# Weight sums of a Strassen feed-forward made earlier and in half-size pieces, and buffers at the change of products given out in order of release

## The chip, the core and the metric

The kernel runs on one core of a Trainium2 chip. TensorE (PE) multiplies matrices into PSUM, VectorE (DVE) and ScalarE (ACT) work on tiles in SBUF, GpSimd (POOL) and SyncE (SP) here mostly issue transfers between device memory and SBUF. Each engine works through its own instructions in the order of the program and waits for others by semaphores. The metric is device time in microseconds.

## The reference

One layer of a hybrid decoder, for 1024 prompt tokens and 8 sample tokens with the same weights; the model width is 1024, the feed-forward width 4096.

```python
y_a, hT_re, hT_im = s5_mixer(u_a, h0_re, h0_im, ...)
v_b = layer_norm(v_b, sgu_ln_g, sgu_ln_b)
y_b = u_b * spatial_mix(v_b, sgu_w, sgu_b)
merged = (jax.nn.sigmoid(gate_a) * (y_a @ w_branch_a)
          + jax.nn.sigmoid(gate_b) * (y_b @ w_branch_b))
mix = merged @ w_out + b_out
x1 = layer_norm(DN_ALPHA * x + mix, ln1_g, ln1_b)
ff = jnp.square(jax.nn.relu(x1 @ w_up + b_up)) @ w_down + b_down
ple = jax.nn.sigmoid(x1 @ w_ple_gate + b_ple_gate) * (p @ w_ple)
x2 = layer_norm(DN_ALPHA * x1 + ff + ple, ln2_g, ln2_b)
```

## The kernel before

Activations are held transposed, 128 features by 1032 tokens to a tile. For precision each operand is split into a high part (written by ACT) and a low part (a DVE subtraction), and a product takes three matmuls. `raw` is a weight tile as it is loaded, `hl` its two parts, `hraw` and `hop` the same for hidden activations that come back from memory.

The program goes through these stages: input projection, state-space scan and gates (to 376 us in the profiled execution); the spatial gating (`sgu_head`, whose last output is `ubt[3]`); `glu`; the merge of the two branches (8 m's, `pab`, evacuated by DVE as `sb` and `sa`); the output projection in two passes over token halves; the gate of the per-layer embedding `pg(0, m)`, then `pg(1, m)`, which also makes the operands `xT`, `xb` of the feed-forward; the up stage from 715 us; the down stage from 1070 us; the last layer norm.

Both feed-forward products are one level of Strassen: seven products instead of eight. In the up stage `up_pair(p)` runs 16 times. Each pair has seven products of 24 matmuls of 128 x 128 x 258 twice; UPO gives their order. ACT or DVE reads each product out of PSUM into `pu`, `p5`, `hA` or `hB`; `hA` and `hB` are squared after a relu, combined into `tA` and `tB`, and stored to `hd` by POOL's queue. Products that share the PSUM region `a` follow each other only after the one ahead is read out. `up_ahead` makes the weights of a coming product: `up_prep` loads both halves of `w_up` and forms the sums (`raw` of 128 x 512), then `split`.

The down stage needs sums of its own weights, S1 to S4, as well. `dn_sums` makes them: for k = 0 to 7 it loads tiles `x`, `y` (`dsum`) and `z` (`dsz`) of 128 x 1024, adds and subtracts four times on DVE, and stores each result with POOL's queue to device memory, from where the down stage loads them. It is a generator: every `next(dsums, None)` in `up_pair` lets it go on for one step. A list scheduler then fixes the order on each engine, so that the order below, not the place in the code, says where an instruction stands.

At the change from up to down, `acc2tags`, `rtags` and `ntags` say which SBUF tiles become the accumulators `acb` (loaded by SP), the four `hraw` buffers and the 23 `hop` tiles. They are taken from a fixed list.

Of the kernel before, what the change touches and what calls it, by code (L numbers as in the profile page):

```python
# [57 lines left out]
def hybrid_step_kernel(ctx: ExitStack, tc: tile.TileContext, i, o):  # L58
# [13 lines left out]
    psb = psb_ctx.enter_context(tc.tile_pool(name="psb", bufs=2, space=PSUM))  # L72
    pools = {"A": ua_pool}

    def unit(tag, dt=F32, shape=None, name=None):
        p = pools["B"] if tag[0] == "B" else pools["A"]
        return p.tile([128, NTOK] if shape is None else shape, dt, tag=tag, name=name or tag)

# [850 lines left out]

# [14 lines left out]
    for m in range(8):  # L944
# [137 lines left out]
    tmpu = unit("T1", name="lnt")  # L1082
    lnx = bpool.tile([128, 1024], F32, tag="dsz", name="lnx")
    xtag = ["B12", "B17", "B18", "B19"]
# [29 lines left out]
    for j, (p_, m) in enumerate(passes):  # L1114
# [63 lines left out]
    for j, m in enumerate(PGO):  # L1178
# [8 lines left out]
        if j % 2:  # L1187
# [24 lines left out]
    def up_prep(n):  # L1212

        p, t = n // 4, n % 4
        if t == 0:
            ra, rb, rc, rd = (raw_() for _ in range(4))
            upr[p] = (ra, rb, rc, rd)
            nc.sync.dma_start(out=ra[:, C5], in_=i["w_up"][p][:, C5])
            nc.sync.dma_start(out=rd, in_=i["w_up"][p + NP])
            nc.sync.dma_start(out=rc[:, D5], in_=i["w_up"][p][:, D5])  # L1220
        ra, rb, rc, rd = upr[p]
        if t == 0:
            tt(V, ra[:, D5], rd[:, C5], rd[:, D5], ALU.add)
# [17 lines left out]


    sd = {n: [dram.tile([128, 1024], F32, tag=f"{n}d{k}", name=f"{n}d{k}") for k in range(8)]
          for n in ("S1", "S2", "S3", "S4")}

    def dn_load(r_, m, j, kh):
        n = 2 * j + kh
        if n == 3:
            nc.sync.dma_start(out=r_, in_=i["w_dl"][m])
        else:  # L1250
            for g in range(2):
                nc.sync.dma_start(out=r_[:, 512 * g:512 * g + 512],
                                  in_=i["w_down"][(2 * n + g) * 4 + m // 2][
                                      :, (m % 2) * 512:(m % 2) * 512 + 512])

    def dn_sums():
        for k in range(8):
            mp, kh = k // 2, k % 2
            x, y = (unit(free[8 + t], F32, [128, 1024], name="dsum") for t in range(2))
            z = bpool.tile([128, 1024], F32, tag="dsz", name="dsz")  # L1260
            dn_load(x, mp + 4, 0, kh)
            dn_load(y, mp + 4, 1, kh)
            dn_load(z, mp, 0, kh)
            for _ in range(5):
                yield
            tt(V, y, x, y, ALU.add)
            nc.gpsimd.dma_start(out=sd["S1"][k], in_=y)  # L1267
            yield
            tt(V, x, z, x, ALU.subtract)
            nc.gpsimd.dma_start(out=sd["S3"][k], in_=x)  # L1270
            yield
            tt(V, z, y, z, ALU.subtract)
            nc.gpsimd.dma_start(out=sd["S2"][k], in_=z)
            y = unit(free[9], F32, [128, 1024], name="dsum")
            dn_load(y, mp, 1, kh)
            for _ in range(3):
                yield
            tt(V, y, y, z, ALU.subtract)
            nc.gpsimd.dma_start(out=sd["S4"][k], in_=y)
            for _ in range(3):  # L1280
                yield

    dsums = dn_sums()

    def up_pair(p):
# [6 lines left out]
        b1, b2 = col("b_up", p), col("b_up", p + NP)  # L1292
        a, c, b = region2(), region2(), region2()
        ps = {"P1": a, "P6": a, "P7": a, "P4": a, "P5": c, "P3": c, "P2": b}
        for nm, t, cs_ in UPO:
            up_ahead(4 * p + t + 3)
            next(dsums, None)
            w = wq[4 * p + t]
# [35 lines left out]
    for p in range(NP):  # L1334
        up_pair(p)


    DNO = ["P1", "P2", "P6", "P7", "P4", "P5", "P3"]
    for _ in dsums:
        pass  # L1340
    pools_free = [f"A{k}" for k in range(16)] + ["T0", "T1"] + [f"B{k}" for k in range(20)]
# [3 lines left out]
    otag = rest[6]  # L1345
    NH = len(ntags)
    acc = []
    for m in range(8):
        u = unit(acc2tags[m], name=f"acb{m}")
        nc.sync.dma_start(out=u, in_=accd[m])  # L1350
        acc.append(u)
    us = [unit(utags[k], F32, [128, 2, HF], name=f"us{k}") for k in range(2)]
    usl = [us[m // 2][:, m % 2] for m in range(4)]
    wn = [0]
# [198 lines left out]
    for n in range(52, 56):  # L1553
# [149 lines left out]
```

## Time and profile before

| | us |
|---|---|
| three runs | 1422.92, 1427.63, 1427.83 |
| median | 1427.63 |
| the profiled execution | 1424.12 |
| its span | 1422.2 |
| PE busy | 1366.1 (96%) |
| DVE busy | 928.8 (65%) |
| ACT busy | 457.1 (32%) |

The mean granted clock of PE was 0.986 of its full speed. Busy time counts the instructions of an engine, without transfers and waits; for PE a busy stretch at a lower granted clock takes longer for the same work.

### The profile page before, as it was taken

How to read it: one execution, taken by the hardware profiler on the slowest of the kernel's cores; microseconds unless marked ns; L12 is line 12 of the kernel's file. 1: busy time of each engine (PE TensorE's matmuls, PEld its weight loads, DVE VectorE, ACT ScalarE, POOL GpSimd, SP SyncE). 2: the span in 40 equal slices, each digit the busy share in tenths (PEclk: the TensorE clock that was granted, in tenths of full speed). 3: DMA queues.
4: the chain of work that ended last, by engine and by line, in shares of the span. 5: the costliest groups of instructions: out<-in, count | busy, mean ns of one | idle time of the engine just before them, and what ended most of it. 6: DMA issues, size and time to landing. Idle time of an engine off the chain costs nothing.

```text
span 1422.2 us, 24852 instructions
## 1 busy us (share of the span) xinstructions
PE 1366.1 (96%) x10302; PEld 1354.6 (95%) x10302; DVE 928.8 (65%) x1488; ACT 457.1 (32%) x616; POOL 143.3 (10%) x214
## 2 busy tenths in 40 slices
PE   8999999999999999999998989999988999999995
PEld 8999899999999999999998979999988999999995
DVE  7929349215765546996887877767756654666857
ACT  3231231133241134562232222223333432344423
POOL 0320310103500000000011212111100000000000
PEclk9999999999999999999999999999998999999998
DMA  7572673531214444423278888644379754665421
GB/s 267 141 187 84 160 151 96 144 136 46 83 57 151 138 123 134 123 88 135 86 249 305 307 277 303 222 158 149 120 262 341 253 159 143 214 214 178 144 81 60
DMA packets 105026, 237.20 MB, mean 167 GB/s; under 512 B 11064, under 2 KB 35528, under 8 KB 104912
## 3 DMA queue, kind: packets, MB, share of 16 engines
q1 hardware_dynamic: 84480, 181.11, 40.2%
q0 software_dynamic: 15344, 51.08, 10.2%
q10 hardware_dynamic: 5088, 3.42, 1.1%
q8 instruction: 81, 1.33, 0.4%
q14 instruction: 33, 0.27, 0.1%
HBM read 160.72 MB, written 68.16 MB: 161 GB/s over the span
## 4 chain that ended last, share of the span: by engine, by line
PE 64%; issue 13%; DVE 12%; DMA 7%; POOL 2%; ACT 1%; SPq 0%; ACTq 0%; POOLq 0%; DVEq 0%
PE q L1077 19%; PE q L1437 18%; PE big L143 11%; DVE tb L83 3%; PE big L120 2%; PE big L122 2%; PE big L121 2%; DMA dsum<-w_down 2%; DVE hl L83 1%; POOL hd L1323 1%; DMA L<-Sst 1%; DMA raw<-w_up 1%; DVE H L83 1%; PE q L1421 1%; PE q L1420 1%
## 5 line engine op out<-in xcount | busy, mean ns | idle before, releaser
L83 DVE TENSOR_TENSOR hl<-raw,hl 128x1024 fp32r<-128x1024 f32 (+1 forms) x189 | 221.5, 1175 | 134.5 <-ACT hl L106 133.6
L106 ACT ACTIVATE hl<-raw 128x1024 fp32r<-128x1024 f32 (+1 forms) x187 | 190.5, 1020 | 324.2 <-PE q L1437 112.5
L1437 PE MATMUL q<-hop,hl 128*128 128x258 f32 x2304 | 280.9, 284 | 4.5 <-DVE hop L1395 3.8
L1437 PEld LDWEIGHTS q<-hop,hl 128*128 128x128 f32 x2304 | 279.8, 191 | 5.3 <-DVE hop L1395 4.0
L1077 PE MATMUL q<-xb,hl 128*128 128x258 f32 x1920 | 241.5, 283 | 0.2 <-ACT p L1307 0.2
L1077 PEld LDWEIGHTS q<-xb,hl 128*128 128x128 f32 x1920 | 235.9, 190 | 0.6 <-ACT p L1307 0.4
L1077 PE MATMUL q<-xT,hl 128*128 128x258 f32 x1536 | 199.2, 289 | 22.0 <-DVE hB L80 21.3
L1077 PEld LDWEIGHTS q<-xT,hl 128*128 128x128 f32 x1536 | 193.3, 195 | 24.2 <-DVE hB L80 22.9
L120 PE MATMUL big<-xh,hl 128*128 128x344 f32 x512 | 165.9, 324 | 1.0 <-ACT uab L293 1.0
L122 PE MATMUL big<-xh,hl 128*128 128x344 f32 x512 | 163.7, 320 | 0.0
L121 PE MATMUL big<-xl,hl 128*128 128x344 f32 x512 | 163.4, 319 | 0.0
L120 PEld LDWEIGHTS big<-xh,hl 128*128 128x128 f32 x512 | 96.2, 188 | 1.8 <-ACT uab L293 1.3
L122 PEld LDWEIGHTS big<-xh,hl 128*128 128x128 f32 x512 | 96.2, 188 | 0.0
L121 PEld LDWEIGHTS big<-xl,hl 128*128 128x128 f32 x512 | 96.2, 188 | 0.0
L1077 PE MATMUL q<-mgh,hl 128*128 128x258 f32 x512 | 83.6, 285 | 1.4 <-DVE sa L83 1.4
L83 DVE TENSOR_TENSOR hop<-hraw,hop 128x516 fp32r<-128x516 f32 x112 | 72.0, 689 | 12.7 <-ACT hop L1397 12.5
L1077 PEld LDWEIGHTS q<-mgh,hl 128*128 128x128 f32 x512 | 71.0, 190 | 1.8 <-ACT hl L106 1.7
L1397 ACT ACTIVATE hop<-hraw 128x516 fp32r<-128x516 f32 x90 | 54.0, 629 | 41.9 <-DMA hraw<-hd 36.4
L83 DVE TENSOR_TENSOR raw<-raw 128x512 f32<-128x512 f32 x64 | 43.3, 688 | 28.4 <-DMA raw<-w_up 28.1
L1077 PE MATMUL q<-mgl,hl 128*128 128x258 f32 x256 | 51.4, 282 | 0.0
L716 ACT ACTIVATE sg<-big,vec 128x1032 f32<-128x1032 f32 x16 | 18.0, 1125 | 96.3 <-issue 55.7
L1267 POOL DMA_DIRECT2D S1d<-dsum x8 | 4.4, 554 | 376.8 <-DVE dsum L83 376.8
(327 smaller groups left out, 1905.7 us busy)
## 6 DMA issues: line engine op xcount, KB each, us to landing
hraw<-hd SPq DMA_DIRECT2D x56, 516.0 KB, 5.1
gd<-sg SPq DMA_DIRECT2D x16, 516.0 KB, 4.0
hd<-hB POOLq DMA_DIRECT2D x16, 516.0 KB, 4.9
hd<-tA POOLq DMA_DIRECT2D x16, 516.0 KB, 5.4
hd<-tB POOLq DMA_DIRECT2D x16, 516.0 KB, 6.0
raw<-w_gate SPq DMA_DIRECT2D x16, 512.0 KB, 4.8
raw<-w_out SPq DMA_DIRECT2D x16, 512.0 KB, 3.6
raw<-w_pg SPq DMA_DIRECT2D x16, 512.0 KB, 3.6
```

The source lines that it names most:

```text
L83: eng.tensor_tensor(out=out, in0=a, in1=b, op=op)
L106: S.activation(out=hi, in_=src, func=AF.Copy)
L120: T.matmul(out, wh, xh[:, sl], start=(start and k == 0), stop=False)
L121: T.matmul(out, wh, xl[:, sl], start=False, stop=False)
L122: T.matmul(out, wl, xh[:, sl], start=False, stop=(stop and k == last))
L143: T.matmul(ps[:, t, 0:TT], w_, x_[:, t * TT:(t + 1) * TT], start=st_, stop=sp_)
L716: S.activation(out=f3(sg), in_=fv(ps), func=AF.Sigmoid, bias=col("b_ga" if m < 8 else "b_gb", m % 8))
L1077: T.matmul(ps[:, j, 0:QT], w_, x_[:, j * QT:(j + 1) * QT], start=st_, stop=sp_, skip_group_check=True)
L1323: put = lambda q, n, src: nc.gpsimd.dma_start(out=d_[q:q + n, p % 2].rearrange("q p n -> p q n"), in_=src)
L1397: S.activation(out=u[:, 0, :], in_=src, func=AF.Copy)
L1420: T.matmul(r_, wh, xl_, start=False, stop=False, skip_group_check=True)
L1437: T.matmul(ps[:, j, 0:QT], w_, x_[:, quarter(j)], start=st_, stop=sp_, skip_group_check=True)
```

## The change

The 32 weight sums become 64 of half the width. They start after the spatial gating, have four buffers of their own (`ds0` to `ds3`), and are stepped in `glu`, in the merge, in the first pass of the output projection and at the ends of up pairs. The `raw` pool goes from four tiles to three; the second half of `w_up` is loaded into `rawu`, in tiles that the per-layer embedding held before. UPO changes; P1 and P2 now both use the weights of step t = 0. Three of the relu-and-square steps go from DVE to ACT, and the first half of `hA` is stored as soon as it is squared. At the change of products, tiles are taken in the order in which the last pair lets go of them, and the `acb` loads go to POOL's queue inside the first `dn_unit`s.

```diff
-    rawp = ctx.enter_context(tc.tile_pool(name="raw", bufs=4))
+    rawp = ctx.enter_context(tc.tile_pool(name="raw", bufs=3))
...
+    def dn_sums():
+        for n in range(16):
+            mp, kh, g = n // 4, n // 2 % 2, n % 2
+            x, y, z, w = (bpool.tile([128, HF], F32, tag=f"ds{t}", name="dsum")[:, 0:512]
+                          for t in range(4))
+            if n == 0:
+                for t in (x, y, z, w):
+                    V.tensor_copy(out=t[:, 0:1], in_=ubt[3][:, 0:1])
+            for t, m, j in ((x, mp + 4, 0), (y, mp + 4, 1), (z, mp, 0), (w, mp, 1)):
+                dn_load(t, m, j, kh, (g,))
+            yield
+            yield
+            tt(V, y, x, y, ALU.add)
+            tt(V, x, z, x, ALU.subtract)
+            tt(V, z, y, z, ALU.subtract)
+            tt(V, w, w, z, ALU.subtract)
+            for nm, t in (("S1", y), ("S3", x), ("S2", z), ("S4", w)):
+                nc.gpsimd.dma_start(out=sd[nm][2 * mp + kh][:, 512 * g:512 * g + 512], in_=t)
+            yield
...
-    UPO = [("P1", 0, C5), ("P5", 0, D5), ("P6", 1, C5), ("P3", 1, D5), ("P7", 2, C5), ("P2", 2, D5),
+    UPO = [("P1", 0, C5), ("P2", 0, D5), ("P6", 1, C5), ("P5", 1, D5), ("P7", 2, C5), ("P3", 2, D5),
            ("P4", 3, D5)]
...
         if t == 0:
-            ra, rb, rc, rd = (raw_() for _ in range(4))
+            ra, rb, rc = (raw_() for _ in range(3))
+            rd = unit(free[8 + p % 2], F32, [128, 1024], name="rawu")
             upr[p] = (ra, rb, rc, rd)
-            nc.sync.dma_start(out=ra[:, C5], in_=i["w_up"][p][:, C5])
+            nc.sync.dma_start(out=ra, in_=i["w_up"][p])
             nc.sync.dma_start(out=rd, in_=i["w_up"][p + NP])
-            nc.sync.dma_start(out=rc[:, D5], in_=i["w_up"][p][:, D5])
...
+            elif nm == "P2":
+                stt(V, h2(hA[:, 0]), r_, b1, h2(p1s), ALU.add, ALU.add)
+                stt(V, hA[:, 0], hA[:, 0], 0.0, hA[:, 0], ALU.max, ALU.mult)
+                put(0, 1, hA[:, 0:1])
+            elif nm == "P7":
+                stt(V, h2(hB[:, 1]), r_, b2, h2(p5), ALU.add, ALU.add)
+                S.activation(out=hB[:, 1], in_=hB[:, 1], func=AF.Relu)
+                S.activation(out=hB[:, 1], in_=hB[:, 1], func=AF.Square)
...
     for p in range(NP):
         up_pair(p)
+        for _ in range(2):
+            next(dsums, None)
...
-    acc2tags = ["A3", "A7"] + [b1tags[1, k] for k in range(4)] + ["B12", "B17"]
-    rest = [t_ for t_ in pools_free if t_ not in acc2tags]
-    utags, rtags, ntags = rest[0:2], rest[2:6], rest[7:]
...
+    rtags = [free[8], free[2], free[3], free[9]]
+    tagof = {id(u): t_ for t_, u in last_of.items()}
+    lasts = [tagof[id(u)] for n in ("11", "21", "T2", "T1", "T3", "22", "T4") for u in xq[n]]
+    NH = 23
+    ntags = lasts[0:NH]
...
+        if pi == 0:
+            if mp == 0:
...
+                acc_in(0)
+            if mp < 3:
+                acc_in(mp + 1)
+            acc_in(mp + 4)
```

The first place is DVE inside an up pair. Before, in the second pair, the four steps of a weight sum (`dsum`, `dsz`) stand among the evacuations `hA`, `hB`:

```order
L83 TENSOR_TENSOR dsum_7371<-dsz_7373,dsum_7371 128x1024
L83 TENSOR_TENSOR dsz_7373<-dsum_7372,dsz_7373 128x1024
L80 SCALAR_TENSOR_TENSOR hA_7181<-q_7188,vec_75,pu_7185 128x516
L83 TENSOR_TENSOR hl_7313<-raw_7249,hl_7313 128x1024
L80 SCALAR_TENSOR_TENSOR hB_7182<-q_7187,vec_75,p5_7186 128x516
L83 TENSOR_TENSOR dsum_7602<-dsum_7602,dsz_7373 128x1024
L80 SCALAR_TENSOR_TENSOR hA_7181<-q_7189,vec_75,pu_7185 128x516
```

With the change the same place of the second pair reads:

```order
L83 SCALAR_TENSOR_TENSOR hA_7294<-q_7302,vec_75,pu_7298 128x516
L83 SCALAR_TENSOR_TENSOR hA_7294<-hA_7294 128x516
L86 TENSOR_TENSOR hl_7364<-raw_7358,hl_7364 128x1024
L86 TENSOR_TENSOR hl_7419<-raw_7359,hl_7419 128x1024
L86 TENSOR_TENSOR raw_7595<-rawu_7597 128x512
L83 SCALAR_TENSOR_TENSOR hB_7295<-q_7300,vec_75,p5_7299 128x516
L86 TENSOR_TENSOR raw_7595<-raw_7595,raw_7594 128x512
L83 SCALAR_TENSOR_TENSOR hA_7294<-q_7301,vec_75,pu_7298 128x516
```

No weight sum is left in it, and the same holds for every pair.

The second place is DVE at the end of `pg(1, m)` and the start of the up stage; `acc3` and `acc7` are the embedding's accumulators of the last two m's. Before:

```order
L83 TENSOR_TENSOR pre3_4572<-pre7_4576,pre3_4572 128x516
L83 TENSOR_TENSOR xT1_3_6879<-pre3_4572,xT1_3_6879 128x516
L83 TENSOR_TENSOR raw_7022<-raw_7025 128x512
L83 TENSOR_TENSOR acc7_5625<-acc7_5625,q_6845 128x516
L83 TENSOR_TENSOR hl_6957<-raw_6942,hl_6957 128x1024
L83 TENSOR_TENSOR acc7_5625<-acc7_5625,q_6859 128x516
```

With the change the sixteenth and last weight sum stands there, and the weights `hl_7067` of the third and fourth products (P6, P5) of the first pair come behind `rawu_7059`:

```order
L86 TENSOR_TENSOR dsum_10056<-dsum_10055,dsum_10056 128x512
L86 TENSOR_TENSOR pre3_4672<-pre7_4676,pre3_4672 128x516
L86 TENSOR_TENSOR xT1_3_7027<-pre3_4672,xT1_3_7027 128x516
L86 TENSOR_TENSOR dsum_10057<-dsum_10057,dsum_10056 128x512
...
L86 TENSOR_TENSOR acc7_5773<-acc7_5773,q_6993 128x516
...
L86 TENSOR_TENSOR raw_7057<-rawu_7059 128x512
L86 TENSOR_TENSOR raw_7058<-raw_7056,rawu_7059 128x512
L86 TENSOR_TENSOR raw_7057<-raw_7057,raw_7056 128x512
L111 CAST xT4_3_7036<-pre7_4676 128x516
L86 TENSOR_TENSOR raw_7058<-raw_7056,raw_7057 128x512
L86 TENSOR_TENSOR xT4_3_7036<-pre7_4676,xT4_3_7036 128x516
L86 TENSOR_TENSOR hl_7067<-raw_7057,hl_7067 128x1024
```

All sixteen sums thus stand ahead of the up stage: sums 0 to 6 from `glu` to the fifth m of the merge, 7 and 8 ahead of the first m of `pg(1, m)`, 9 to 15 one in each of its first seven m's. The loads of `rawu` stand on SP like this, behind the last store of an embedding tile but one:

```order
L1233 DMA accd3_5777<-acc3_5769 128x1032
L1267 DMA rawu_7133<-w_up 128x1024
L1267 DMA rawu_7059<-w_up 128x1024
L1233 DMA accd7_5781<-acc7_5773 128x1032
L1266 DMA raw_7130<-w_up 128x1024
```

Both `rawu` tiles lie where the operands `ph1` and `pl1` of the last embedding product were, so both loads wait for PE's last matmul ahead of the up stage.

The third place is DVE in the last up pair. Before, the evacuation of P7 (`hB`) has three splits of `hop` ahead of it in that pair, from two `hraw` tiles:

```order
L83 TENSOR_TENSOR hop_10575<-hraw_10573,hop_10575 128x516
L80 SCALAR_TENSOR_TENSOR hA_10358<-q_10365,vec_75,pu_10362 128x516
L83 TENSOR_TENSOR hop_10578<-hraw_10573,hop_10578 128x516
L83 TENSOR_TENSOR hl_10674<-raw_10671,hl_10674 128x1024
L83 TENSOR_TENSOR hop_10587<-hraw_10581,hop_10587 128x516
L80 SCALAR_TENSOR_TENSOR hB_10359<-q_10364,vec_75,p5_10363 128x516
```

With the change it has twelve splits from six `hraw` tiles ahead of it, these the last of them:

```order
L86 TENSOR_TENSOR hop_10749<-hraw_10731,hop_10749 128x516
L1407 CAST hop_10752<-hraw_10731 128x516
L86 TENSOR_TENSOR hop_10757<-hraw_10739,hop_10757 128x516
L86 TENSOR_TENSOR hop_10752<-hraw_10731,hop_10752 128x516
L86 TENSOR_TENSOR hop_10760<-hraw_10739,hop_10760 128x516
L86 TENSOR_TENSOR hl_10826<-raw_10823,hl_10826 128x1024
L83 SCALAR_TENSOR_TENSOR hB_10511<-q_10516,vec_75,p5_10515 128x516
```

Four `hraw` buffers serve six loads there, so the last two loads wait for splits of the first four.

## Rows read from the trace of the kernel before

**Rows 1.** Page, busy time of each engine: us, share of the span, instructions.

```profile
PE 1366.1 (96%) x10302; PEld 1354.6 (95%) x10302; DVE 928.8 (65%) x1488; ACT 457.1 (32%) x616; POOL 143.3 (10%) x214
```

**Rows 2.** What PE waited for: us in total, times, the longest.

```profile
PE q L1077 <- DVE hB L80: 21.3, 8, 5.2
...
PE q L1437 <- DVE hop L1395: 3.8, 1, 3.8
...
PE q L1437 <- DVE hop L83: 0.7, 1, 0.7
```

**Rows 3.** Timeline, ACT, evacuation that ends a pair: start us, duration, idle before.

```profile
736.20 0.70 ACT L1318 ACTIVATE hB<-q,vec 128x516 f32<-128x516 f32 x1 [1.83 <-PE q L1077]
...
902.25 0.69 ACT L1318 ACTIVATE hB<-q,vec 128x516 f32<-128x516 f32 x1 [5.96 <-PE q L1077]
...
1043.74 0.70 ACT L1318 ACTIVATE hB<-q,vec 128x516 f32<-128x516 f32 x1 [1.78 <-PE q L1077]
...
1069.81 0.69 ACT L1318 ACTIVATE hB<-q,vec 128x516 f32<-128x516 f32 x1 [1.69 <-PE q L1077]
```

**Rows 4.** Timeline, PE, one stall in the up stage.

```profile
851.05 4.47 PE L1077 MATMUL q<-xT,hl 128*128 128x258 f32 x24 [5.17 <-DVE hB L80]
```

**Rows 5.** Timeline, PE, the first product of the up stage.

```profile
715.10 3.05 PE L1077 MATMUL q<-xb,hl 128*128 128x258 f32 x24
```

**Rows 6.** Windows of 20 us, two in the up stage.

```profile
835.00:855.00 20.00, 14.82 (x112) 14.62 (x111) 13.64 (x18) 3.63 (x4) 3.79 (x6) 0.91 0.79 264
...
915.00:935.00 20.00, 20.00 (x168) 20.00 (x167) 13.60 (x17) 5.99 (x8) 2.69 (x4) 1.00 0.44 155
```

**Rows 7.** Timeline, DVE, ahead of the stall of rows 4.

```profile
838.16 1.29 DVE L83 TENSOR_TENSOR raw<-raw 128x512 f32<-128x512 f32 x2
843.18 0.69 DVE L83 TENSOR_TENSOR raw<-raw 128x512 f32<-128x512 f32 x1 [3.72 <-DMA raw<-w_up]
843.79 1.22 DVE L83 TENSOR_TENSOR dsum<-dsum 128x1024 f32<-128x1024 f32 x1
...
850.25 0.75 DVE L80 SCALAR_TENSOR_TENSOR hB<-q,vec,p 128x516 f32<-128x516 f32 x1
```

**Rows 8.** Window of 5 us at the start of the down stage.

```profile
1085.00:1090.00 5.00, 4.42 (x22) 4.42 (x23) 4.63 (x6) 1.72 (x4) 0.00 (x0) 0.54 1.04 398
```

**Rows 9.** Transfers, 920 to 1020 us: KB each, median us to landing.

```profile
raw<-w_up SPq DMA_DIRECT2D x10, 256.0 KB, 2.6
raw<-w_up SPq DMA_DIRECT2D x5, 512.0 KB, 3.6
hd<-hA POOLq DMA_DIRECT2D x5, 258.0 KB, 2.8
```

**Rows 10.** Transfers, 760 to 860 us.

```profile
dsum<-w_down SPq DMA_DIRECT2D x16, 256.0 KB, 4.5
...
hd<-hA POOLq DMA_DIRECT2D x5, 258.0 KB, 3.2
```

**Rows 11.** Window of 20 us in the merge.

```profile
430.00:450.00 20.00, 20.00 (x129) 20.00 (x128) 9.87 (x9) 4.25 (x4) 0.00 (x0) 1.00 0.38 123
```

**Rows 12.** Timeline, DVE, one evacuation of two following m's of the merge.

```profile
422.23 1.23 DVE L83 TENSOR_TENSOR sa<-big,sa 128x1032 f32<-128x1032 f32 x1 [4.39 <-PE big L143]
...
433.56 1.23 DVE L83 TENSOR_TENSOR sa<-big,sa 128x1032 f32<-128x1032 f32 x1 [4.31 <-PE big L143]
```

**Rows 13.** Window of 20 us in pg(1, m).

```profile
665.00:685.00 20.00, 20.00 (x168) 20.00 (x167) 16.39 (x24) 4.55 (x6) 0.00 (x0) 1.00 0.35 129
```

**Rows 14.** Timeline, DVE, the accumulations of two following m's of pg(1, m).

```profile
662.52 1.38 DVE L83 TENSOR_TENSOR acc<-acc,q 128x516 f32<-128x516 f32 x2
...
671.21 1.38 DVE L83 TENSOR_TENSOR acc<-acc,q 128x516 f32<-128x516 f32 x2
```

**Rows 15.** Timeline, DVE, the first accumulation of acc7.

```profile
713.85 0.69 DVE L83 TENSOR_TENSOR acc<-acc,q 128x516 f32<-128x516 f32 x1 [0.55 <-PE q L1077]
```

**Rows 16.** Transfers, 1040 to 1100 us.

```profile
hraw<-hd SPq DMA_DIRECT2D x14, 516.0 KB, 6.7
```

More of the change, by code (lines that the diff above doesn't have):

```diff
@@ L73, in hybrid_step_kernel @@
     pools = {"A": ua_pool}
+    last_of = {}
     def unit(tag, dt=F32, shape=None, name=None):
         p = pools["B"] if tag[0] == "B" else pools["A"]
-        return p.tile([128, NTOK] if shape is None else shape, dt, tag=tag, name=name or tag)
+        u = p.tile([128, NTOK] if shape is None else shape, dt, tag=tag, name=name or tag)
+        last_of[tag] = u
+        return u
     def stt(eng, out, in0, sc, in1, op0, op1):
@@ L908, in hybrid_step_kernel, with dn_load @@
         tt(V, ubt[h], sgt[h], ubt[h], ALU.mult)
+    sd = {n: [dram.tile([128, 1024], F32, tag=f"{n}d{k}", name=f"{n}d{k}") for k in range(8)]
+          for n in ("S1", "S2", "S3", "S4")}
+    def dn_load(r_, m, j, kh, gs=(0, 1)):
+        n = 2 * j + kh
+        if n == 3:
+            c = slice(512 * gs[0], 512 * gs[-1] + 512)
+            nc.sync.dma_start(out=r_, in_=i["w_dl"][m][:, c])
+        else:
+            for k, g in enumerate(gs):
+                nc.sync.dma_start(out=r_[:, 512 * k:512 * k + 512],
+                                  in_=i["w_down"][(2 * n + g) * 4 + m // 2][
+                                      :, (m % 2) * 512:(m % 2) * 512 + 512])
+    def dn_sums():
[17 more added lines that the diff above has]
+            yield
+    dsums = dn_sums()
     yhl += [(unit(f"A{8 + 2 * m}", F32R, name=f"yh{m + 2}"), unit(f"A{9 + 2 * m}", F32R, name=f"yl{m + 2}"))
@@ L956, in hybrid_step_kernel @@
         mg.append((a, b))
+        next(dsums, None)
     half = lambda p_: slice(p_ * HF, (p_ + 1) * HF)
@@ L1082, in hybrid_step_kernel @@
     tmpu = unit("T1", name="lnt")
-    lnx = bpool.tile([128, 1024], F32, tag="dsz", name="lnx")
     xtag = ["B12", "B17", "B18", "B19"]
@@ L1127, in hybrid_step_kernel @@
         if p_ == 0 and m == 7:
+            next(dsums, None)
+            next(dsums, None)
+            lnx = bpool.tile([128, HF], F32, tag="ds0", name="lnx")
             lnq.add(ln_half(pre, 0, ssum, tmpu, lnx, "ln1_g", "ln1_b", x1_split))
@@ L1130, in hybrid_step_kernel @@
             lnq.pull(1)
+        elif m < 7:
+            next(dsums, None)
     lnq.drain()
@@ L1240, in hybrid_step_kernel @@
     ptags, htags = free[0:2], (free[2:4] + free[6:8], free[4:6] + free[6:8])
[L1243 to L1283, printed above, removed]
     def up_pair(p):
@@ L1293, in up_pair @@
         a, c, b = region2(), region2(), region2()
+        d_ = hd[p // 2]
+        put = lambda q, n, src: nc.gpsimd.dma_start(
+            out=d_[q:q + n, p % 2].rearrange("q p n -> p q n"), in_=src)
         ps = {"P1": a, "P6": a, "P7": a, "P4": a, "P5": c, "P3": c, "P2": b}
@@ L1296, in up_pair @@
             up_ahead(4 * p + t + 3)
-            next(dsums, None)
             w = wq[4 * p + t]
@@ L1335, in hybrid_step_kernel @@
         up_pair(p)
+        for _ in range(2):
+            next(dsums, None)
     DNO = ["P1", "P2", "P6", "P7", "P4", "P5", "P3"]
@@ L1340, in hybrid_step_kernel, with acc_in @@
         pass
-    pools_free = [f"A{k}" for k in range(16)] + ["T0", "T1"] + [f"B{k}" for k in range(20)]
-    acc2tags = ["A3", "A7"] + [b1tags[1, k] for k in range(4)] + ["B12", "B17"]
-    rest = [t_ for t_ in pools_free if t_ not in acc2tags]
-    utags, rtags, ntags = rest[0:2], rest[2:6], rest[7:]
[L1345 to L1348, printed above, removed]
+    rtags = [free[8], free[2], free[3], free[9]]
[3 more added lines that the diff above has]
+    ntags = lasts[0:NH]
+    rest = lasts[NH:]
+    acc2tags = [free[0], free[1], free[4], free[5], free[6], free[7]] + rest[0:2]
+    utags, otag = rest[2:4], rest[4]
+    acc = [None] * 8
+    def acc_in(m):
         u = unit(acc2tags[m], name=f"acb{m}")
[L1350 to L1353, printed above, removed]
+        nc.gpsimd.dma_start(out=u, in_=accd[m])
+        acc[m] = u
+    us, usl = [], []
     wn = [0]
@@ L1425, in dn_unit @@
         ps = region2()
+        if pi == 0:
+            if mp == 0:
+                us.extend(unit(utags[k], F32, [128, 2, HF], name=f"us{k}") for k in range(2))
+                usl.extend(us[k // 2][:, k % 2] for k in range(4))
+                acc_in(0)
+            if mp < 3:
+                acc_in(mp + 1)
+            acc_in(mp + 4)
         for k in range(16):
@@ L1477, in hybrid_step_kernel @@
     perm = [4, 5, 6, 7, 0, 1, 2, 3]
-    accp = [acc[m] for m in perm]
     def ln_last(t0, n, step_):
         sl = slice(t0, t0 + n)
-        xs_ = [s_[:, sl] for s_ in accp]
+        xs_ = [acc[m][:, sl] for m in perm]
         a, b, x = (tmp2[:, k * TT:k * TT + n] for k in range(3))
@@ L1539, in hybrid_step_kernel @@
     tmp2 = unit(utags[1], name="lnt2")
-    lnx = bpool.tile([128, 1024], F32, tag="dsz", name="lnx")
+    lnx = bpool.tile([128, HF], F32, tag="ds0", name="lnx")
     lnq.add(ln_half(acc, 0, sum2, tmp2, lnx, "ln2_g", "ln2_b", ln2_out))
@@ L1557, in hybrid_step_kernel @@
         wdn[n] = (a, b)
-    ones5 = bpool.tile([128, 1024], F32, tag="dsz", name="ones5")[:, 0:128]
+    ones5 = bpool.tile([128, HF], F32, tag="ds1", name="ones5")[:, 0:128]
     V.memset(ones5, 1.0 / 640.0)
```

24 lines of the change are left out of this document (8 added, 16 removed).

## The prediction

> **What bounds the kernel now.** Read first the page: PE is busy for 1366.1 of 1422.2 us [rows 1], so only what keeps PE waiting, or slows it, can give time back. The waits of PE say where: 21.3 us in eight waits in the up stage for DVE's evacuation `hB`, and 3.8 and 0.7 us for `hop` [rows 2]. The instruction that waits is P4, which adds to the PSUM region that P7 must first be read out of.
>
> Next read the ends of the pairs [rows 3]. From 902.25 to 1043.74 there are seven pairs of 20.21 us, none disturbed. The seven from 736.20 to 902.25 took 166.05 instead of 141.47: 24.6 us lost. The last took 26.07: 5.9 lost. That is more than the waits alone, because PE's clock falls behind a long wait: behind 5.17 us the 24 matmuls of a product took 4.47 us [rows 4], against 3.05 at the full clock [rows 5]. Such a wait costs some 1.4 us more.
>
> Why DVE is late in pairs 1 to 7 is seen in two windows [rows 6]. In 835 to 855 the transfers keep their engines busy for 0.79 of the time, at 264 GB/s; in 915 to 935, without weight sums, for 0.44 at 155 GB/s, and there DVE needs only 13.60 of 20 us. DVE waits 3.72 us for a `w_up` load, then works through what is queued, weight sums of 1.22 us among it, and reaches `hB` at 850.25 [rows 7]. Neither a full DVE nor a full PE, but waits for transfers in one queue of DVE instructions.
>
> At the change of products PE waits 4.5 us [rows 2], and in 1085 to 1090 it is granted 0.54 of its clock [rows 8]: 4.42 busy x 0.46 is 2.0 us more. So 24.6 + 5.9 + 4.5 + 2.0 = 37.0 us lie open. The sum below is made against the profiled execution, 1424.1 us, which is 3.5 under the median of 1427.6.
>
> **The sums leave the up stage.** All sixteen stand ahead of it, so no pair has their four DVE steps nor their loads and stores. ACT gets five passes of a 128x516 tile, 0.70 us each [rows 3], 3.5 us in all; it was busy for 5.99 of 20 [rows 6]. DVE loses work. Pairs 1 to 7 should then look like pairs 8 to 14: **-24.6**. Half of a pair's DVE time as cover is ample; gone, it would cost what pairs 1 to 7 cost now.
>
> **Sums 3 to 6 in the merge.** DVE is busy 9.87 of 20 us there and the transfers 0.38 [rows 11], so four steps more per m find room. A 128x512 step is priced by `raw`: 1.29 for two, 0.65 each [rows 7]. But each tile has one buffer: store, load, then the next sum. Call store plus load R. In the calm stretch a 258 KB store took 2.8 and a 256 KB load 2.6 [rows 9], R = 5.4; in the busy one 3.2 and 4.5 [rows 10], R = 7.7. From a sum's first step to the store of `x` DVE does that step, three passes of 1.22 (`sa`, `hl`, `sa`) and the second step, 5.0; the cycle is 5.0 + R. An m takes 11.33 [rows 12]. At 5.4 the cycle is 10.4 and fits; at 7.7 it is 12.7, 1.4 late per m, 5.6 over four m's, and the second PSUM region covers one product, 5.7. I take **+1**, 0 to 4. Behind a waiting step stand `sa` and `sb`, for which PE's region waits. Sums 0 to 2 fall where DVE has gaps, 7 and 8 ahead of the first accumulation of `pg(1, m)`: within that +1.
>
> **Sums 9 to 15 in pg(1, m).** An m takes 8.69 us [rows 14]. DVE is busy 16.39 of 20 [rows 13], 7.12 per m; with four steps 9.7. That is 1.0 too much, seven times; the eighth m has no sum and gives 1.6 back: DVE is 5.4 us late at the start of the up stage. PE has a whole m of products in further PSUM regions, 8.69, less 2.5 for the evacuation itself, so some 6 us of cover. The buffer cycle (first step, a pass of 1.22, second step) is 2.5 + R: 7.9 or 10.2 against 9.7, so R matters above 7.2 only. At 7.7 the lateness grows by 3.5 to 9, 3 above the cover. **+1**, 0 to 6.
>
> **The first up pair.** P1 and P2 use one weight tile, ready early, and take 2 x 2.89 us (a seventh of 20.21). Call their start T, 715.10 before [rows 5]. P6 needs `hl_7067`, made from `rawu_7059`, whose load waits for PE's last matmul ahead of T. A 512 KB load took 3.6 [rows 9]; two are issued together, and 256 KB more cost 1.0 there, so the second lands between T+3.6 and T+5.6. From there DVE has three `raw` steps, `xT4`, another `raw`, `xT4` and the split: some 4.5 to 5. That alone is T+10, a stall of 4. DVE's own lateness adds: the first accumulation of `acc7` began at 713.85 [rows 15], T-1.25; 5.4 late is T+4.2, and eight passes (six of 0.65, 1.22, 0.42) stand ahead of the `raw` steps, so T+9.7 and the split done by T+14, a stall of 8. Taking DVE as some 3 late, because PE's own small waits give some back, the stall is 5.6 and the clock's fall 1.4: **+7**, between 4 and 10. Before, nothing waited here.
>
> **The change of products.** Tiles come free in order, so four `hraw` loads can go out in the last pair, and the `acb` loads no longer stand ahead on SP. But DVE now has twelve splits of six `hraw` tiles ahead of P7's `hB`, in place of three. Four buffers serve six loads. A first load of 6.7 us [rows 16], splits, a second of 6.7 and four more splits bring DVE to about 17.5 us into the pair, then `hl` 1.22 and `hB` 0.75: 19.5. P4 could start at six products, 17.3. A stall of 2 to 4, and 1.4 for the clock, say 5; then up to 3 at the first down product, say 2. So 7 of the 12.4 stay: **-5.5**, between 0 and -12.4. `raw` with three tiles costs nothing that I can see: in every stage two loads can still run ahead of the split in work, and if that cover failed once, a load of 3.6 is the price.
>
> Sum: 1424.1 - 24.6 + 1 + 1 + 7 - 5.5 = 1403.0. Half of the distance to the median, 1.75, is added: **1404 us**, about 23 under the median.
>
> **Rivals.**
>
> *Both new waits are hidden.* DVE isn't late in pg(1, m), `rawu` lands early, `hraw` loads run ahead of the splits. For it: each new wait rests on a few us of lateness. Against: the `rawu` load has no way to be early. Full gain is 1424.1 - 37.0 = 1387, with 3 for P6 at least 1390. Chance 0.17.
>
> *The change of products gives nothing.* The `hraw` waits only move from P1 of the down stage to P4 of the last up pair, for the transfers are full there anyway (6.7 us per load). Then the sum is 1403 + 5.5, about 1409. Chance 0.15.
>
> *The buffers' round trip holds DVE.* One mechanism: R above the break-even (7.2 in pg(1, m), and in the merge 6.3 plus a quarter of 5.7, 7.7). Each us above it costs seven and four us. If stores land like the busy loads, R = 9.0: 7 x 1.8 + 4 x 1.3 = 18, some 1422, no difference to tell. For it: small pieces, one buffer each, DVE in order. Against: the transfers were busy 0.38 of the time in the merge, not 0.79. Chance 0.08. It decides against the change from R = 9.9 on, where 11 R - 81 reaches the 28 us that make 1403 into 1431. At R = 10.5 it is 1438, slower; loads of this size had a median of 4.5 even in the busy stretch [rows 10], so only stores that hold each other up on POOL's queue would make it so. Chance 0.06. The Trainium skill bears on this: "DMA: Bandwidth & Descriptors", section "Bandwidth", advises transfers of 1 MiB and more, and the section "Anatomy of one DMA" gives some 2.0 us fixed plus the bytes at 436 GB/s. By that estimate R is 5.2 and this rival falls away, while a halved piece pays the fixed part twice; the trace agrees on the size of a single transfer (2.6 for 256 KB, 3.6 for 512 KB).
>
> **How the numbers follow.** The forecast's own case, 1396 to 1412, has 0.54. Faster by over 0.5% (7 us, about what a measurement here can tell from no change) hold it, the hidden waits and the change that gives nothing: 0.54 + 0.17 + 0.15 = 0.86. Within 0.5%: 0.08. Slower: 0.06. The range has to leave out no more than 2 in 10: down to 1389, nearly the full gain, and up to 1421, where the round trip at R = 9.0 begins to eat all.
>
> **What would show it.** Pairs 1 to 14 at 20.21 us with no wait of PE for `hB`: the first term. One wait of PE at the third product of pair 0, for `hl` or `raw`, 4 to 8 us long: the third. In the merge and in pg(1, m) PE without waits over 1 us, DVE busy 18 to 20 of 20 in pg(1, m), and little idle time ahead of `dsum`; if DVE waits there for the loads of `dsum`, the round trip is the story. At the change a PE wait of 2 to 4 us for `hB` in the last pair, and less than 3 at the start of the down stage. The prediction is wrong if pairs other than the first and last still wait, or if the merge takes longer than 8 x 11.33.

## The result and the profile after

The changed kernel takes 1432.25 us (median of eight runs), the kernel before 1424.86 on the same chips: ratio 1.0054, 95% interval 1.004 to 1.0069. It is slower by about half a per cent, where the prediction had it 23 us faster. The profiled execution, 1433.99 us, lies 1.7 above the median; its span is 1432.2 us, 10.0 more than before, and the rows below add up to this 10.0.

The page of the changed kernel, busy time of each engine, against [rows 1]:

```profile
PE 1372.2 (96%) x10302; PEld 1361.1 (95%) x10302; DVE 904.7 (63%) x1508; ACT 503.0 (35%) x696; POOL 166.7 (12%) x254
```

DVE lost 24 us of work and ACT gained 46, and PE does the same matmuls. What PE waits for, against [rows 2]:

```profile
PE q L1120 <- ACT acc L1197: 12.3, 2, 8.9
PE big L146 <- DVE sa L86: 9.2, 4, 2.5
...
PE q L1120 <- ACT pu L1314: 3.9, 1, 3.9
PE q L1457 <- DVE hl L86: 3.4, 1, 3.4
PE q L1120 <- ACT hl L109: 2.7, 1, 2.7
```

The eight waits of 21.3 us for `hB` are gone. In their place stand two for `acc`, in `pg(1, m)`, and four for `sa`, in the merge. The ends of the pairs on ACT, against [rows 3]:

```profile
773.94 0.69 ACT L1328 ACTIVATE hB<-q,vec 128x516 f32<-128x516 f32 x1 [0.64 <-PE q L1120]
...
1036.53 0.69 ACT L1328 ACTIVATE hB<-q,vec 128x516 f32<-128x516 f32 x1 [0.64 <-PE q L1120]
...
1056.73 0.69 ACT L1328 ACTIVATE hB<-q,vec 128x516 f32<-128x516 f32 x1 [0.65 <-PE q L1120]
```

Pairs 1 to 14 take 282.79 us, 20.20 each, 24.7 less than before. But the first pair ends 37.7 us later than before. The stages ahead of it are told apart by PE's first matmul of the output projection and of the up stage. Before, the output projection began here (the up stage: [rows 5]):

```profile
502.90 0.48 PE L1077 MATMUL q<-mgh,hl 128*128 128x258 f32 x2 [1.42 <-DVE sa L83]
```

and in the changed kernel here, followed by P1 and P2 of the first pair in one row, and by P6 of that pair:

```profile
518.43 0.48 PE L1120 MATMUL q<-mgh,hl 128*128 128x258 f32 x2 [1.42 <-DVE sa L86]
...
748.64 5.92 PE L1120 MATMUL q<-xb,hl 128*128 128x258 f32 x48
757.30 1.24 PE L1120 MATMUL q<-xT,hl 128*128 128x258 f32 x8 [2.74 <-ACT hl L109]
```

| stretch | forecast | measured, by these rows |
|---|---|---|
| to the end of the merge | +1 | 518.43 - 502.90 = +15.5 |
| to the start of the up stage | +1 | 748.64 - 715.10 - 15.5 = +18.0 |
| first pair | +7 | 773.94 - 736.20 - 33.5 = +4.2 |
| pairs 1 to 14 | -24.6 | 1056.73 - 1043.74 - 37.7 = -24.7 |
| last pair and down stage | -5.5 | 10.0 - 13.0 = -3.0 |

**The merge.** DVE there, one m and the start of the next:

```profile
428.97 0.69 DVE L86 TENSOR_TENSOR dsum<-dsum 128x512 f32<-128x512 f32 x1 [5.33 <-DMA dsum<-w_down]
429.58 1.22 DVE L86 TENSOR_TENSOR sa<-big,sa 128x1032 f32<-128x1032 f32 x1
...
433.00 1.41 DVE L86 TENSOR_TENSOR dsum<-dsum 128x512 f32<-128x512 f32 x2
...
444.40 0.69 DVE L86 TENSOR_TENSOR dsum<-dsum 128x512 f32<-128x512 f32 x1 [7.10 <-DMA dsum<-w_down]
445.00 1.23 DVE L86 TENSOR_TENSOR sa<-big,sa 128x1032 f32<-128x1032 f32 x1
```

From `sa` to `sa` it is 15.42 us, where [rows 12] have 11.33. DVE stands 7.10 us for a load with `sa` behind it. The store of `x` on POOL's queue, and the next loads on SP's (three, 439.59 the first):

```profile
433.98 0.54 POOL L946 DMA_DIRECT2D S3d<-dsum  x1 [3.48 <-DVE dsum L86]
```

```profile
439.59 4.43 SPq L925 DMA_DIRECT2D dsum<-w_down  x3
```

So the store takes 5.6 us from issue until the load of the next `x` may go out, and the load 4.8 until DVE's step at 444.40: a round trip of 10.4 us, where the prediction reckoned with 5.4 to 7.7. The transfers between 410 and 490 us, against [rows 9, 10] (KB each, median us to landing), and one window of 20 us there, against [rows 11]:

```profile
dsum<-w_down SPq DMA_DIRECT2D x16, 256.0 KB, 3.9
...
sa<-gd SPq DMA_DIRECT2D x5, 516.0 KB, 6.5
...
S3d<-dsum POOLq DMA_DIRECT2D x6, 256.0 KB, 5.1
...
S1d<-dsum POOLq DMA_DIRECT2D x5, 256.0 KB, 2.3
```

```profile
430.00:450.00 20.00, 16.76 (x89) 16.48 (x90) 12.83 (x15) 3.19 (x3) 3.21 (x6) 0.86 0.60 194
```

The store of `y` (S1d) lands in 2.3 us in three of five cases: there it goes out after DVE has stood waiting, 2.0 us ahead of the next load. That of `x` (S3d) goes out with the loads of `raw`, `sb` and `sa`, which DVE steps within 3 us of it let go, and with the store of `z` 0.7 us behind it, and takes 5.1 in the median. Two further stores of `y` went out at the same time as a load, at 419.54 and 447.40, and took 5.4 and 4.7. The burst thus goes with the slow stores; whether the loads or the stores behind slow them wasn't separated.

PE's granted clock in this window is 0.86. The first late product and a product of the same matmuls a little later:

```profile
430.86 1.23 PE L146 MATMUL big<-yah,hl 128*128 128x344 f32 x3 [2.51 <-DVE sa L86]
...
434.32 0.63 PE L146 MATMUL big<-yal,hl 128*128 128x344 f32 x3
```

Between these two rows the granted clock is 0.53. The four waits come to 9.2 us in all; most of the rest of the 15.5 is this lower clock behind the first three of them.

**pg(1, m).** DVE, where sums 8 and 9 meet:

```profile
667.31 2.87 DVE L86 TENSOR_TENSOR dsum<-dsum 128x512 f32<-128x512 f32 x4 [3.12 <-DMA dsum<-w_down]
...
676.41 0.69 DVE L86 TENSOR_TENSOR dsum<-dsum 128x512 f32<-128x512 f32 x1 [2.62 <-DMA dsum<-w_down]
677.02 0.69 DVE L86 TENSOR_TENSOR pre<-pre 128x516 f32<-128x516 f32 x1
681.26 0.69 DVE L86 TENSOR_TENSOR dsum<-dsum 128x512 f32<-128x512 f32 x1 [3.54 <-DMA dsum<-w_down]
```

ACT at the same time:

```profile
677.75 0.64 ACT L109 ACTIVATE xT<-pre 128x516 fp32r<-128x516 f32 x1 [9.02 <-DVE pre L86]
685.29 0.63 ACT L109 ACTIVATE xT<-pre 128x516 fp32r<-128x516 f32 x1 [6.91 <-DMA accd<-acc]
685.83 1.04 ACT L109 ACTIVATE hl<-raw 128x1024 fp32r<-128x1024 f32 x1
686.77 0.67 ACT L1197 ACTIVATE acc<-q,vec 128x516 f32<-128x516 f32 x1
```

and PE:

```profile
687.50 8.67 PE L1120 MATMUL q<-xb,hl 128*128 128x258 f32 x48 [8.86 <-ACT acc L1197]
...
728.60 8.61 PE L1120 MATMUL q<-xb,hl 128*128 128x258 f32 x48 [3.46 <-ACT acc L1197]
```

DVE waits for loads of `dsum` with `pre` behind them; ACT waits for `pre` and for an embedding store, with the read-out `acc` of a PSUM region behind them; PE waits for that region, and then runs 48 matmuls in 8.67 us, at a granted clock of 0.64 (687 to 696 us); at 1.00 (699 to 705 us) they take 5.96. The two waits for `acc`, 12.3 us, and 5.4 us for the clock behind them make up nearly all of the 18.0. The chain passes through two engines' order.

### The profile page after: what moved, and what is told of

Its sections match the earlier page's. It is cut to its first block, busy times and chain, and to the rows that moved or that the text cites. A ratio compares the mean times of both kernels' runs of the same rounds, so it can differ in the third digit from the quotient of the medians.

```text
span 1432.2 us, 25009 instructions
## 1 busy us (share of the span) xinstructions
PE 1372.2 (96%) x10302; PEld 1361.1 (95%) x10302; DVE 904.7 (63%) x1508; ACT 503.0 (35%) x696; POOL 166.7 (12%) x254
## 3 DMA queue, kind: packets, MB, share of 16 engines
q0 software_dynamic: 17008, 55.31, 10.9%
## 4 chain that ended last, share of the span: by engine, by line
PE 45%; issue 33%; DVE 11%; DMA 5%; POOL 4%; ACT 1%; SPq 0%; ACTq 0%; POOLq 0%; DVEq 0%
PE q L1457 18%; PE q L1120 8%; PE big L146 3%; DVE tb L86 3%; PE big L123 2%; PE big L125 2%; PE big L124 2%; POOL hd L1298 2%; DMA L<-Sst 1%; DVE H L86 1%; DVE hl L86 1%; PE q L1431 1%; PE q L1432 1%; PE q L1433 1%; DMA raw<-w_down 1%
## 5 line engine op out<-in xcount | busy, mean ns | idle before, releaser
L86 DVE TENSOR_TENSOR hl<-raw,hl 128x1024 fp32r<-128x1024 f32 (+1 forms) x173 | 210.6, 1221 | 204.8 <-ACT hl L109 204.6
L109 ACT ACTIVATE hl<-raw 128x1024 fp32r<-128x1024 f32 x171 | 180.4, 1056 | 252.3 <-PE q L1457 112.3
L1120 PE MATMUL q<-xb,hl 128*128 128x258 f32 x1920 | 243.5, 287 | 12.4 <-ACT acc L1197 12.3
L1120 PEld LDWEIGHTS q<-xb,hl 128*128 128x128 f32 x1920 | 239.0, 194 | 13.2 <-ACT acc L1197 12.7
L1120 PE MATMUL q<-xT,hl 128*128 128x258 f32 x1536 | 193.5, 286 | 7.1 <-ACT pu L1314 3.9
L1120 PEld LDWEIGHTS q<-xT,hl 128*128 128x128 f32 x1536 | 189.9, 192 | 7.9 <-ACT pu L1314 4.1
L86 DVE TENSOR_TENSOR dsum<-dsum 128x512 f32<-128x512 f32 x64 | 44.1, 688 | 49.2 <-DMA dsum<-w_down 47.1
L83 DVE SCALAR_TENSOR_TENSOR hA<-q,vec,pu 128x516 f32<-128x516 f32 x32 | 24.1, 755 | 44.8 <-issue 27.5
```

The costliest lines, as they stand in the source:

```text
L83: eng.scalar_tensor_tensor(out=out, in0=in0, scalar=sc, in1=in1, op0=op0, op1=op1)
L86: eng.tensor_tensor(out=out, in0=a, in1=b, op=op)
L109: S.activation(out=hi, in_=src, func=AF.Copy)
L1120: T.matmul(ps[:, j, 0:QT], w_, x_[:, j * QT:(j + 1) * QT], start=st_, stop=sp_, skip_group_check=True)
```

## The experiments

**Theory A.** Each tile of the weight sums has one buffer, so a sum must be stored and the next loaded before DVE can go on, and DVE, in order, holds `sa`, `sb` and `pre` behind that wait. Rivals: the three `raw` tiles or the new order of products (B), DVE's added steps (C), the sheer volume of transfers (D). Runs 2 to 4 and 8 to 10 are one execution each.

**Runs 1 to 4: where the sums stand, and what their cycle is.** So that the scheduler can't draw a sum forward, its first step takes a factor of one that is made from a tile of the wanted place:

```diff
-            tt(V, y, x, y, ALU.add)
+            one = bpool.tile([128, 1], F32, tag="one", name="one")
+            ts(V, one, tie[0], 0.0, 1.0, ALU.mult, ALU.add)
+            stt(V, y, x, one[:, 0:1], y, ALU.mult, ALU.add)
```

Run 1 has every sum in the up stage, one to a pair:

> The changed kernel, with every weight sum held back into the up stage, one per pair: its first step takes a factor of one that is made from that pair's hA, so that it can't stand earlier. The same transfers, steps and four buffers. Theory A (in the merge and in pg(1, m) DVE, in order, waits for the store and reload of a sum's single buffers): the merge goes back to 11.33 us per m and pg(1, m) to 8.69, pairs stay at 20.2, since a round trip of some 10 us fits into a pair; about 1400 us, 33 less than the change. Theory B (the three raw tiles, or the new order of products, cost the time ahead of the up stage): the merge stays near 15 us per m and the time near 1432.

Measured: 1408.1 us, ratio to the kernel before 0.9869 (0.9841 to 0.9897). `sa` follows `sa` at 11.33 us, the up stage has no waits of PE in pairs 1 to 14. B falls for the time ahead of the up stage: the `raw` tiles and the order of products are the changed kernel's. Pairs 1 to 14 run from 741.09 to 1023.89 us, 20.20 each, with the sums in them. The gain is smaller than expected: two sums fall into the last pair, and PE waits 10.9 us for weights at the start of the down stage.

Runs 2, 3 and 4 put eight sums into the merge, one per m; in run 2 a second factor of one, made from `sa`, holds the later steps behind sa + sb:

> The changed kernel with one weight sum in each of the eight m's of the merge, its four steps spread over the m as the change has them in four of the m's (first step ahead of sa, the others behind sa + sb), and the other eight sums one per pair in the up stage. A control for the next two. Theory A: a cycle of 5.0 us of DVE work plus a round trip of some 10.4 us, so about 15.4 us per m in all eight m's, the merge some 30 us longer than before; pg(1, m) at 8.69 us per m.

> As e2, but the eight sums of the merge are not stored, and the down stage loads weights of the same size in place of all sums, so the output is not the reference's. DVE's steps and the loads stay where they are. Theory A: without the store a reload may start at once, the cycle is 5.0 + 4.8 = 9.8 us, below 11.33: the merge takes 11.33 us per m, 30 us less than e2. Rival C (DVE's added steps and their places are what delays sa and sb): still some 15 us per m. Rival D (transfers at the limit of their bandwidth): in between, since half of the sums' bytes are gone.

> As e2, with the four steps of a sum one behind the other, behind sb. Same steps, loads and stores. Theory A: from the first step to the store of x only 1.3 us of DVE work in place of 5.0, so a cycle of 1.3 + 10.4 = 11.7 us, or less if the stores land sooner; about 11.3 to 12 us per m, the merge 0 to 5 us longer than before. Rivals C and D: 15 us per m, as e2.

| run | sums in the merge | us from `sa` to `sa` | us in all |
|---|---|---|---|
| 2 | eight, steps spread | 13.7 to 15.6 | 1426.3 |
| 3 | eight, spread, not stored | 11.33 | 1397.1 |
| 4 | eight, steps packed | 11.33, from the fifth m on 11.5 to 12.4 | 1407.7 |

The first step of a sum on DVE in run 2, then in run 3 with the `sa` behind it, then in run 4 with its three followers and `sa`:

```profile
449.48 0.75 DVE L83 SCALAR_TENSOR_TENSOR dsum<-dsum,one 128x512 f32<-128x512 f32 x1 [5.42 <-DMA dsum<-w_down]
```

```profile
431.17 0.75 DVE L83 SCALAR_TENSOR_TENSOR dsum<-dsum,one 128x512 f32<-128x512 f32 x1 [1.09 <-DMA dsum<-w_down]
433.12 1.23 DVE L86 TENSOR_TENSOR sa<-big,sa 128x1032 f32<-128x1032 f32 x1 [1.19 <-PE big L146]
```

```profile
430.36 0.75 DVE L83 SCALAR_TENSOR_TENSOR dsum<-dsum,one 128x512 f32<-128x512 f32 x1
431.14 2.15 DVE L86 TENSOR_TENSOR dsum<-dsum 128x512 f32<-128x512 f32 x3
434.44 1.23 DVE L86 TENSOR_TENSOR sa<-big,sa 128x1032 f32<-128x1032 f32 x1 [1.15 <-PE big L146]
```

In run 2 DVE waits for the load, in run 3, and in run 4 up to the fourth m, `sa` waits for PE, as before. Run 2 costs less than expected: its output projection begins at 524.24 us, 21.3 later than before, where 30 were expected, and its m's are mostly below 15.4 us. Runs 3 and 4 came out as expected by theory A. Run 3 has DVE's steps in the same places, so C falls. Run 4 has the same steps, loads and stores as run 2, so D falls: what differs is that the later steps follow the first at once, so that the time from the first step to the store of `x` is 1.3 us in place of some 5. That the cycle of single buffers is the cost in the merge is shown; why its round trip is 10.4 us is read from rows of the change and not tested by itself.

**Run 5: what a round trip may take.** Four sums in the merge, in every second m and packed, twelve in pairs 1 to 12:

> The changed kernel with four weight sums in the merge, one in every second m, packed behind sb, and the other twelve one per pair in pairs 1 to 12. Theory A: every second m gives a sum's buffers 22.7 us for a round trip of some 10, so the merge stays at 11.33 us per m; pg(1, m) at 8.69; no sum stands in the last pair, where the first experiment had a wait of 10.9 us for weights. About 1397 to 1402 us, some 26 under the kernel before. If the waits for the sums' buffers aren't the whole cost, it stays above 1410.

Measured: 1401.0 us, ratio 0.9825 (0.9803 to 0.9846), `sa` to `sa` 11.33, pairs of 20.2, as expected. The place decides, not the half-size pieces.

**Run 6: the first pair.**

```diff
+            if p == 0:
+                rd = [bpool.tile([128, HF], F32, tag=f"ds{t}", name="rawd")[:, 0:512] for t in (2, 3)]
+            else:
+                u = unit(free[8 + p % 2], F32, [128, 1024], name="rawu")
+                rd = [u[:, C5], u[:, D5]]
```

> As the four-and-twelve version, but the second half of w_up of the first pair is loaded into two of the sums' tiles, so that this load doesn't wait for PE's last matmul ahead of the up stage. If that load is what the third product of the first pair waits for (2.7 to 3.6 us and the clock behind it): 4 to 5 us less, and no wait of PE at the start of the up stage. If DVE's own lateness is the cause: no difference.

Measured: 1395.2 us, ratio to the kernel before 0.9789 (0.9769 to 0.9809), 5.8 less than run 5. PE at the start of the up stage in run 5 and then in run 6:

```profile
714.79 5.92 PE L1134 MATMUL q<-xb,hl 128*128 128x258 f32 x48
723.84 11.42 PE L1134 MATMUL q<-xT,hl 128*128 128x258 f32 x72 [3.13 <-ACT hl L109]
```

```profile
715.74 5.92 PE L1134 MATMUL q<-xb,hl 128*128 128x258 f32 x48
721.50 8.82 PE L1134 MATMUL q<-xT,hl 128*128 128x258 f32 x72
```

Run 5 waits 3.13 us for the weights of the third product, and its next 72 matmuls take 2.6 us longer; run 6 has neither. The granted clock over the 72 matmuls is 0.75 in run 5 and 1.00 in run 6. So the load of `rawu` behind PE's last matmul was the cause.

**Run 7: the change of products.**

```diff
-    rtags = [free[8], free[2], free[3], free[9]]
...
+    rest = [t_ for t_ in pools_free if t_ not in acc2tags]
+    utags, rtags, ntags = rest[0:2], rest[2:6], rest[7:]
```

> As the four-and-twelve version, but the buffers at the change of feed-forward products come from the fixed list of the kernel before, and acb is loaded on SP's queue ahead of them. If giving out tiles in order of release and moving the acb loads is what shortened the change: 2 to 6 us more, with PE waits for hop of some 4 us at the start of the down stage, and no wait for pu in the last pair. If the two are worth nothing: the same time.

Measured: 1409.1 us, 8.1 more than run 5, more than expected. PE's wait at the start of the down stage, run 7 and then run 5:

```profile
1077.77 32.44 PE L1463 MATMUL q<-hop,hl 128*128 128x258 f32 x249 [11.40 <-ACT hl L109]
```

```profile
1064.90 45.33 PE L1466 MATMUL q<-hop,hl 128*128 128x258 f32 x353 [2.88 <-DVE hl L86]
```

It waits for weights (`hl`), not for `hop` as expected. The lists with the `acb` loads are worth 8.1 us with this order of products; which of the two brings it wasn't separated. In the profiled execution with the old lists the time from the end of the fifteenth pair (1023.08 us) to the end of the span is 384.3 us, against 378.5 before and 375.5 in run 5: something else in the change costs some 6 us there, and the lists give back more than that. Whether it is the three `raw` tiles, which the prediction put at nothing, no run shows. A wait in the last pair stays with either, 3.4 us for `pu` in run 5 and 2.9 for `p` in run 7.

**Runs 8 to 10: pg(1, m).** Seven sums there, packed, one behind each accumulation; then two more ahead of the first, as the change has them; then run 8 without stores:

```diff
         nc.sync.dma_start(out=accd[m], in_=acc[m])
+        sum_at(acc[m][:, 0:1])
```

> The changed kernel with seven weight sums in pg(1, m), one behind each of the accumulations of m 1 to 7, packed, none in the merge, nine in the up stage. Theory A: DVE needs 9.7 us per m against 8.69 and the buffers' cycle is 1.3 + some 7.6: pg(1, m) longer by 5 to 10 us in place of the 18 of the change, where sums 7 and 8 stood back to back ahead of it. If the transfers as such hold it: 18 or more.

> The changed kernel's arrangement in pg(1, m) alone: two weight sums back to back ahead of its first accumulation, then one behind each of the first seven, none in the merge, seven in the up stage. Theory A with its burst: the two sums ahead put eight stores and eight loads beside the weights and the embedding's stores, DVE waits for the third sum's loads, and ACT, in order behind it, reads PSUM late: pg(1, m) 10 us or more longer than in the version with seven sums and none ahead (3.5 us), towards the 18.0 of the change, with one PE wait for acc of 5 to 9 us. Rival: if the waits follow from DVE's sum of work alone, two steps ahead of the stage add at most their own 4.9 us.

> As the version with seven sums in pg(1, m), but those seven are not stored, and the down stage loads weights of the same size in place of all sums, so the output is not the reference's. Theory A: without stores the loads land early, pg(1, m) returns to 8.69 us per m, and what is left is DVE's work, 9.7 us per m against 8.69, up to 5 us of lateness at the first pair. If the 11.6 us that the seven sums cost to the end of the first pair are DVE's work, they stay.

Measured from the start of the output projection to the end of the first pair (before: 736.20 - 502.90 = 233.3; run 5, without sums there: 238.5):

| kernel | us | against run 5 |
|---|---|---|
| run 8, seven sums | 250.1 | +11.6 |
| run 9, two ahead and seven | 256.5 | +18.0 |
| run 10, seven, not stored | 242.2 | +3.7 |
| the change | 255.5 | +17.0 |

The ends of the first pair in runs 5, 8, 9 and 10, in this order (their output projections begin at 502.60, 502.60, 502.73 and 502.40 us):

```profile
741.06 0.69 ACT L1339 ACTIVATE hB<-q,vec 128x516 f32<-128x516 f32 x1 [0.64 <-PE q L1134]
...
752.67 0.68 ACT L1337 ACTIVATE hB<-q,vec 128x516 f32<-128x516 f32 x1
...
759.23 0.68 ACT L1342 ACTIVATE hB<-q,vec 128x516 f32<-128x516 f32 x1
...
744.62 0.69 ACT L1337 ACTIVATE hB<-q,vec 128x516 f32<-128x516 f32 x1 [0.64 <-PE q L1131]
```

In runs 1, 3, 5 and 7, none of which has sums in pg(1, m), this stretch takes 237.4 to 238.8 us, so about 1 us tells nothing. (In runs 2 and 4, where the output projection begins behind a late merge, it is 241.2 and 242.3.)

In run 9 PE waits for `acc` as in the changed kernel:

```profile
670.37 8.16 PE L1131 MATMUL q<-xb,hl 128*128 128x258 f32 x48 [7.47 <-ACT acc L1204]
```

In run 8 most of the lateness reaches PE only in the first pair, at P6:

```profile
735.32 11.25 PE L1131 MATMUL q<-xT,hl 128*128 128x258 f32 x72 [9.46 <-ACT hl L109]
```

PE's up stage begins at 714.8 in run 5, at 719.1 in run 8 and at 730.3 in run 9. So pg(1, m) itself is 4.3 us longer with seven sums, a little less than expected, and 15.5 with the two ahead, as expected. In run 10 pg(1, m) is undisturbed and the first pair waits 6.9 us:

```profile
714.58 5.92 PE L1131 MATMUL q<-xb,hl 128*128 128x258 f32 x48
727.37 11.44 PE L1131 MATMUL q<-xT,hl 128*128 128x258 f32 x72 [6.87 <-ACT hl L109]
```

So of run 9's 18.0 us DVE's own work and the loads are 3.7, the stores and the reloads behind them 7.9, and the two sums back to back 6.4. The rival of run 9, at most 4.9 for these two, does not hold for the stage (11.2); at the end of the pair the 6.4 exceeds it by 1.5, hardly more than the spread. That the two sums act through a burst of transfers is argued from the rows above and not separated.

## Why the prediction was wrong

- **The sums leave the up stage, -24.6:** right in size, -24.7; 20.20 us per pair. That the sums had to leave for it is not shown: run 1 has one half-size sum in each of pairs 1 to 14, and they take 20.20 us too. Whether half the sums' work per pair, the new order of products or the steps moved to ACT frees the pairs wasn't separated.
- **Sums 3 to 6 in the merge, +1 (0 to 4):** wrong, +15.5. The form was right, a cycle of 5.0 us and the round trip R, and its price was not: R was 10.4. The step that failed is the choice of R from landing times of other stretches (5.4 to 7.7). In the merge the store goes out in the same few us as three loads of 512 to 516 KB that DVE lets go. The clock behind PE's waits, priced for the first and the last pair, was put at nothing here and in pg(1, m); it was some 5 us in each. The mean share of 0.38 that was put against the rival said nothing of that.
- **Sums 9 to 15 in pg(1, m), +1 (0 to 6):** wrong, +18.0. The cover of 6 us in PSUM regions was not there: ACT, which reads them out, waits in order for `pre` behind the same DVE steps. Sums 7 and 8 were put to "within that +1", and run 9 against run 8 prices two sums ahead at 6.4. For R in pg(1, m) there is no figure of its own.
- **First pair, +7 (4 to 10):** 4.2 in the change, with a wait of 2.7 in place of 5.6; right in cause. Run 6 shows that the late `rawu` load is all of it where no sums stand ahead: 5.8 us. The lateness of DVE that was to add to it did not show in the change, where PE itself had been held up; it shows in runs 8 and 10, with waits of 9.5 and 6.9 us. That the term came within its bounds is thus partly luck.
- **Change of products, -5.5:** -3.0. The wait in the last pair is 3.9 us, in the forecast 2 to 4, but for `pu` on ACT and not for DVE's `hB`: ACT, in order, has the high parts of `hop` ahead of that read-out and waits for their `hraw` loads. And 3.4 us for `hl` stay behind the change.

```profile
1070.92 0.63 ACT L1409 ACTIVATE hop<-hraw 128x516 fp32r<-128x516 f32 x1 [2.04 <-DMA hraw<-hd]
1071.46 0.58 ACT L1314 ACTIVATE pu<-q 128x516 f32<-128x516 f32 x1
```

- **The rivals:** the one that came true is the buffers' round trip, with 0.06 for slower. Its deciding point, R = 9.9 in the merge and in pg(1, m), was near: 10.4 in the merge. The sign that the prediction named for itself, a merge longer than 8 x 11.33 us, came. Half-size pieces as such cost nothing in run 5. By the fit for transfers that GpSimd issues in the Trainium skill, "DMA: Bandwidth & Descriptors", section "Anatomy of one DMA", a 256 KB store is estimated at 2.6 us. The store of `y` took 2.3 in the median, that of `x`, beside others, 5.1, so the estimate does not hold for the latter; the loads here are issued by SP, for which that section gives no fit.

## What to carry to other kernels

A chain of one buffer (compute, store, load, compute) on an engine that works in order can't be priced by landing times of calmer stretches or by the mean share of the transfers in its stage; look at what else is let go in the same few us. Here the round trip was about twice the quiet one (10.4 against 5.4). Give the chain a period that holds this and the work between its first step and its store, keep its steps together, and place it where nothing urgent stands behind its wait. Before reckoning with PSUM as cover, follow the engine that reads it out through its own order. This kernel's list scheduler drew the sums forward out of the output projection and the up pairs: what is meant for a certain stage needs a dependency on that stage.

## What the runs showed of the hardware

A 256 KB store took 2.3 us when it went out ahead of the next loads and 5.1 in the median beside three larger loads, in one stage of one kernel. And the clock nearly doubled the price of a wait: behind 3.13 us of waiting in the first pair, 72 matmuls took 11.42 us in run 5, at a granted clock of 0.75, and 8.82 in run 6, at 1.00, where nothing had waited; of the 5.8 us between the two runs the wait is about half.
